# Gates in seven products behind the attention's projection, and a state-space layer cut into tables and a main part

## The chip, the cores and the metric

The kernel runs on one core of a Trainium2 chip. TensorE (PE) multiplies matrices into PSUM; VectorE (DVE), ScalarE (ACT) and GpSimd (POOL) do the elementwise work; transfers are issued from the queues of SP, ACT and POOL. Every engine takes its instructions in the order in which the program emits them, and waits on semaphores for what other engines produce. The metric is the time of one execution in microseconds of the device. Before the change it is 2796.81 us, the median of 3 runs (2796.46 to 2797.84).

## The reference

One decoder block in float32. 16 learned tokens are put before 512 tokens of width 2048, so 528 rows go in and 512 come out.

```python
n = rms_norm(h, norm_mix[l])
z = n @ w_in[l]
q_lat, kv_lat, k_r, u, gates = jnp.split(z, [OFF_Q, OFF_KV, OFF_KR, OFF_U], axis=-1)
...
attn_out = attn @ w_attn_proj[l]
y = s5_scan(u.reshape(bsz, length, SSM_GROUPS, SSM_GROUP), ...)
y = jax.nn.gelu(y.reshape(bsz, length, SSM_WIDTH).astype(h.dtype))
ssm_out = (y @ w_glu_val[l]) * jax.nn.sigmoid(y @ w_glu_gate[l])
mixed = jax.nn.sigmoid(g[:, :, 0]) * attn_out + jax.nn.sigmoid(g[:, :, 1]) * ssm_out
h = h + mixed @ w_out[l]
m = rms_norm(h, norm_ffn[l])
h = h + (jax.nn.silu(m @ w_ffn_gate[l]) * (m @ w_ffn_up[l])) @ w_ffn_down[l]
```

The widths that matter here: u has 1024 columns, q_lat and kv_lat 512 each, the rotated key 64 (128 in the kernel's form), the gates 4096. The attention has 16 heads; the state-space layer has 64 groups of 16 channels and 64 complex states. The output is the final norm of h without the learned tokens.

## The kernel before

**Precision and units.** Activations and weights are each split into a high and a low part (`hilo`, L317; `Weights._split`, L261 and L262), ScalarE making the high part and VectorE the low one. A product is three matmuls: high by high, high by low, low by high. Weights come in blocks of 128 x 1024, that is eight k tiles of one column tile, on SP's queue. One block is one unit of TensorE: 8 k tiles x 3 matmuls. `Weights.use` (L279) splits two blocks ahead of TensorE; the parts lie in rings of three buffers, and the blocks as loaded in `wraw`, a ring of three, which in the seven-product stages is joined by H0 to H3 and H6.

**Two forms.** `dense` (L369) is the plain form: 16 k tiles in two units for one column tile. `seven` (L1353) multiplies a 2 x 2 arrangement of half-size blocks with seven products instead of eight: for one column tile of two (512 tokens, 16 k tiles by 2 column tiles) seven units of 24 matmuls with 256 columns, named P1, P5, P6, P2, P7, P3, P4. VectorE builds weight sums for it (`_combine`, L228); the activations are needed in the forms XD, B12, XA, T12 and T34. The first pair of a stage is `plain_pair` (L1509), four units of 24 matmuls with 512 columns or their halves, during which the operands of the sevens are split. `gathered` (L1381) brings the seven products of a pair together.

**Stages.** (1) Input norm and split of x. (2) Eight tiles of u, 528 wide, stored in DRAM (`ud`). (3) Four tiles of kv, one of the rotated key (kr), four of q, then 32 plain tiles of the gates, whose sigmoids go to DRAM (`sg`). (4) The attention, head by head in an order written out by hand (`TURN`). (5) Its projection, 16 plain tiles, each multiplied with its gate. (6) The two GLU products from y, gated and merged. (7) The output projection. (8) The FFN, gate and up in sevens. (9) Down in three parts, two of which begin with a plain pair. (10) The final norm.

**Work beside the matmuls.** `dense` calls `bg` (L354) behind every unit. It first runs what stands in `later` with a count that has come down to zero, and then steps a generator, `ssm` (L510), as long as there is credit: each call adds 3.6 and each step subtracts the cost that it yields. Credit never rises above 3.6. `ssm` makes the state-space layer's parameters and then, for each of four blocks of 16 groups, its tables and its results: a Toeplitz table (`kd`, then TT), the input expansion transposed for TensorE (BT), the rotations (ER), the powers of the output side (CLt), then states, rotation, scan, rotation back, and outputs y, which go to DRAM (`yd`). It starts with kv and is finished by `bg(1e9)` behind the gates. `by_group` (L496) moves halves of a tile between partitions with transfers on ACT's queue.

**What sets the order around the change.** On each engine the order is the emitted one, so a small matmul of `ssm` stands between two units of TensorE, and a waiting instruction holds up all behind it. On POOL's queue stand the transfers of u, y, kd, the gates and the operands; a transfer into a buffer waits until the last reader of what lay there is done. PSUM has two buffers A, two B, and one each of D, Q and V; the attention's first products take them in turns (`up_ps`, L877). The key's rotation needs the transfers kcs and krs, the queries' rotation (`up_rope`, L883) the tables cs.

## Time and profile before

| what | us |
|---|---|
| median of 3 runs | 2796.81 |
| the profiled execution | 2798.5 |
| its span, first to last instruction | 2796.7 |
| TensorE busy | 2753.9 (98%) |
| VectorE busy | 1908.9 (68%) |
| ScalarE busy | 1136.4 (41%) |
| GpSimd busy | 414.5 (15%) |
| first and last gate tile stored | 231.3 and 611.3 |
| attention's projection, first matmul | 906.3 |
| a stretch of the FFN's sevens, 1510 to 2305: TensorE busy | 795.0 of 795 |

Rows of the profile are read so. A group: line, engine, operation, out<-in by tile names, partitions x elements, count, then total busy time and mean ns of one, then the idle time in front of it and what ended it. A row of the chain or the timeline: start, length, what, count. A row of stretches: from and to, length, busy time with count for PE, PEld, DVE, ACT and POOL, then TensorE's granted clock, the share of the DMA engines and GB/s. A row of transfers: out<-in, queue, count, size, time from issue to landing. Matmul durations of one instruction overlap with the next, so the pace of a unit is read from the chain.

### The profile page before, as it was taken

How to read it: one execution, taken by the hardware profiler on the slowest of the kernel's cores; microseconds unless marked ns; L12 is line 12 of the kernel's file. 1: busy time of each engine (PE TensorE's matmuls, PEld its weight loads, DVE VectorE, ACT ScalarE, POOL GpSimd, SP SyncE). 2: the span in 40 equal slices, each digit the busy share in tenths (PEclk: the TensorE clock that was granted, in tenths of full speed). 3: DMA queues.
4: the chain of work that ended last, by engine and by line, in shares of the span. 5: the costliest groups of instructions: out<-in, count | busy, mean ns of one | idle time of the engine just before them, and what ended most of it. 6: DMA issues, size and time to landing. Idle time of an engine off the chain costs nothing.

```text
span 2796.7 us, 47538 instructions
## 1 busy us (share of the span) xinstructions
PE 2753.9 (98%) x19654; PEld 2537.8 (91%) x19654; DVE 1908.9 (68%) x2609; ACT 1136.4 (41%) x1625; POOL 414.5 (15%) x633
## 2 busy tenths in 40 slices
PE   9999999999999999999999999999999999999997
PEld 8988788889998888888889999999999998999997
DVE  6467556556666333343578888888888888788896
ACT  5123222235555332232234444444444445353445
POOL 2012222231111000111212000000000002030202
PEclk9999999999999999999999999999999999999999
DMA  5334454552122343334434434343433336474542
GB/s 193 107 117 118 136 150 118 146 145 69 61 65 61 125 139 112 114 117 143 143 114 140 139 129 151 112 145 129 143 135 122 136 133 253 168 261 167 206 156 99
DMA packets 114632, 378.88 MB, mean 135 GB/s; under 512 B 16720, under 2 KB 21584, under 8 KB 114352
## 3 DMA queue, kind: packets, MB, share of 16 engines
q1 hardware_dynamic: 76672, 263.36, 27.7%
q0 software_dynamic: 36320, 109.29, 12.4%
q10 hardware_dynamic: 1424, 3.21, 0.5%
q8 instruction: 154, 2.52, 0.4%
q14 instruction: 62, 0.51, 0.1%
HBM read 316.04 MB, written 51.97 MB: 132 GB/s over the span
## 4 chain that ended last, share of the span: by engine, by line
PE 91%; DVE 3%; DMA 2%; issue 2%; ACT 1%; POOL 0%; DVEq 0%; ACTq 0%; POOLq 0%
PE psA L315 60%; PE psB L315 19%; PE psQ L315 5%; PE psV L315 4%; PE psD L315 1%; DVE wlo L262 1%; DVE S L322 1%; DMA S<-td 0%; DMA raw<-in_wst 0%; DVE ev L322 0%; PE psA L1028 0%; ACT whi L261 0%; DMA T<-td 0%; DMA ssB<-td 0%; DMA H<-td 0%
## 5 line engine op out<-in xcount | busy, mean ns | idle before, releaser
L315 PE MATMUL psA<-S,whi 128*128 128x256 f32 (+2 forms) x5440 | 1305.6, 327 | 16.9 <-ACT whi L261 6.5
L315 PEld LDWEIGHTS psA<-S,whi 128*128 128x128 f32 x5440 | 920.1, 188 | 115.8 <-ACT whi L261 7.9
L315 PE MATMUL psA<-S,wlo 128*128 128x256 f32 (+2 forms) x2720 | 889.6, 327 | 1.0 <-DVE wlo L262 0.9
L262 DVE TENSOR_TENSOR wlo<-raw,whi 128x1024 fp32r<-128x1024 f32 (+1 forms) x479 | 592.8, 1239 | 296.0 <-ACT whi L261 293.7
L261 ACT ACTIVATE whi<-raw 128x1024 fp32r<-128x1024 f32 (+1 forms) x479 | 504.3, 1055 | 533.9 <-PE psA L315 254.8
L315 PEld LDWEIGHTS psA<-S,wlo 128*128 128x128 f32 x2720 | 512.7, 189 | 48.9 <-DVE wlo L262 1.6
L315 PE MATMUL psB<-S,whi 128*128 128x256 f32 (+1 forms) x1392 | 285.0, 283 | 0.1
L262 DVE TENSOR_TENSOR wlo<-cmb,whi 128x1024 fp32r<-128x1024 f32 x180 | 220.0, 1222 | 67.4 <-ACT whi L261 66.3
L261 ACT ACTIVATE whi<-cmb 128x1024 fp32r<-128x1024 f32 x180 | 190.5, 1058 | 177.6 <-DVE wlo L262 124.9
L315 PEld LDWEIGHTS psB<-S,whi 128*128 128x128 f32 x1392 | 227.2, 189 | 0.3 <-PE psD L315 0.3
L315 PE MATMUL psB<-S,wlo 128*128 128x256 f32 (+1 forms) x696 | 195.9, 281 | 1.6 <-DVE wlo L262 1.6
L315 PEld LDWEIGHTS psB<-S,wlo 128*128 128x128 f32 x696 | 131.5, 189 | 1.8 <-DVE wlo L262 1.8
L1316 POOL DMA_DIRECT2D td<-sC x22 | 15.8, 720 | 755.8 <-ACT ev L1388 711.9
L242 DVE TENSOR_TENSOR cmb<-raw,raw 128x1024 f32<-128x1024 f32 x60 | 73.2, 1219 | 10.5 <-DMA raw<-in_wst 10.5
L322 DVE TENSOR_TENSOR H<-psA,ev 128x512 f32<-128x512 f32 x32 | 22.1, 691 | 85.2 <-PE psA L315 85.2
L840 ACT ACTIVATE ev<-ev 128x512 f32<-128x512 f32 x32 | 20.2, 632 | 147.6 <-DVE ev L322 147.5
L322 POOL TENSOR_TENSOR acc<-acc,ev 128x512 f32<-128x512 f32 (+2 forms) x43 | 53.4, 1241 | 162.6 <-ACT ev L1619 80.6
L315 PE MATMUL psA<-H,whi 128*128 128x264 f32 (+2 forms) x312 | 76.5, 334 | 0.7 <-DVE ev L322 0.5
L242 DVE TENSOR_TENSOR cmb<-cmb,raw 128x1024 f32<-128x1024 f32 x60 | 73.3, 1221 | 0.0
L242 DVE TENSOR_TENSOR cmb<-raw,cmb 128x1024 f32<-128x1024 f32 x60 | 73.2, 1220 | 0.0
L242 DVE TENSOR_TENSOR raw<-raw,raw 128x1024 f32<-128x1024 f32 x60 | 73.1, 1219 | 0.0
L315 PE MATMUL psB<-ssA,whi 128*128 128x256 f32 (+1 forms) x340 | 72.5, 303 | 0.0
(630 smaller groups left out, 4906.7 us busy)
## 6 DMA issues: line engine op xcount, KB each, us to landing
raw<-in_wst SPq DMA_DIRECT2D x485, 512.0 KB, 3.6
td<-sC POOLq DMA_DIRECT2D x22, 512.0 KB, 3.2
td<-H POOLq DMA_DIRECT2D x40, 256.0 KB, 3.3
S<-td POOLq DMA_DIRECT2D x40, 256.0 KB, 7.4
sg<-ev POOLq DMA_DIRECT2D x32, 256.0 KB, 2.3
ev<-sg POOLq DMA_DIRECT2D x32, 256.0 KB, 2.9
U<-ER POOLq DMA_DIRECT2D x64, 64.0 KB, 2.0
ev<-in_xT POOLq DMA_DIRECT2D x16, 256.0 KB, 2.9
```

Of the source, the lines that this page charges most:

```text
L242: self.nc.vector.tensor_tensor(t, g(a), g(b), op=op)
L261: self.nc.scalar.activation(hi[:, a:b], w[:, a:b], AF.Copy)
L262: self.nc.vector.tensor_tensor(lo[:, a:b], w[:, a:b], hi[:, a:b], op=ALU.subtract)
L315: PE.matmul(o, lhsT=l, rhs=r, start=start, stop=stop, skip_group_check=more)
L322: eng.tensor_tensor(o, a, b, op=op)
L840: ACT.activation(e, e, AF.Sigmoid)
L1316: POOL.dma_start(td[pr, 0:2].rearrange("f p n -> p f n"), Cu)
```

## The change

The gates leave the first stages. Their weights move in the stream behind those of the attention's projection, ordered by pairs: the pair of a column tile of the attention's gate and the same tile of the state-space gate. The first pair is plain, the other 15 are sevens. Their operands are made from x again: `x_products` loads x, multiplies with gain and norm factor and stores the forms to DRAM (`xd`), beside the attention's projection. The projection's tiles go to DRAM (`ao`) and are multiplied with their gates in the gates stage.

The state-space layer is cut in two. `ssm_first` makes parameters and tables for all four blocks, with an allowance of 4.0 a unit, from behind the second tile of u on, and keeps them in DRAM (`bd`, `ed`, `kd`, `cd`), but for the last block's powers. C is loaded without its zero columns and multiplied once for all blocks; the first 18 rotations are computed for all blocks at once. What is left of it behind kr is emitted at once by `run_out`. `ssm_main` runs beside the attention's projection with one step a unit: it loads the tables, makes the last powers, and computes states, scan and outputs; the Gelu is applied as the outputs leave PSUM. `bg` now steps a list of generators, each with its own allowance and credit.

The order of the first stages becomes u, q, kv, kr. The kv norm is started behind kr's first unit and all its pieces behind the second; the key's rotation is finished behind the queries' first rotation. The last GLU operands are loaded and split during the last gate pair. In the down projection the first pairs' weights go through the eight raw buffers (kind Q), and all T12 operands are loaded at P6 of the pair before.

`seven`, `gathered`, `plain_pair`, `Operands` and `products` move ahead in the file, with `Operands` taking its source and `products` its destination as arguments. The core of the diff:

```diff
+N_FIRST = 94
+N_GATES = 4 * KT
...
-    it = [("P", b) for b in range(N_PLAIN)]
+    it = [("P", b) for b in range(N_FIRST)] + [("Q", N_FIRST + b) for b in (0, 2, 1, 3)]
+    for q in range(1, N_GATES // 4):
+        it += [("S", N_FIRST + 4 * q, u) for u in range(7)]
+    it += [("P", b) for b in range(N_FIRST + N_GATES, N_PLAIN)]
...
-                it += [("P", d + b) for b in (0, 2, 1, 3)]
+                it += [("Q", d + b) for b in (0, 2, 1, 3)]
...
+            if it[0] == "Q":
+                self.loads.append((i, i, it[1], self.RAW[nraw % 8]))
+                nraw += 1
+            elif it[0] != "S":
...
+        for g in list(bg_gens):
+            g[1] = min(g[1] + g[2], g[2])
+            while g[1] > 0:
+                try:
+                    g[1] -= next(g[0])
+                except StopIteration:
+                    bg_gens.remove(g)
+                    break
+
+    def beside(gen, allow):
+        bg_gens.append([gen, 0.0, allow])
+
+    def run_out():
+        for g in bg_gens:
+            for _ in g[0]:
+                pass
+        bg_gens.clear()
...
+    def ssm_tables(b):
+
+
+        js, g0 = slice(b * BP, (b + 1) * BP), b * BG
+        Bt = sb([P, 2, BP, 16], F32, "sw")
+        POOL.dma_start(Bt, A["sb"][:, :, js])
+        Dg = sb([P, BG * 16], F32, "sK")
+        POOL.dma_start(Dg, A["sd"][:, g0 * 16:(g0 + BG) * 16])
+        T1 = sb([P, 2 * T], F32, "T1")
+        T2 = sb([P, 2 * T], F32, "T2")
+
+        C, C48 = tabs["C"], tabs["C48"]
+        for ph, c in ((slice(0, P), 0), (RH[0], 16), (RH[1], 32)):
+            ACT.activation(C48[ph, :, :, c:c + 16], C[ph, :, js], AF.Copy)
+
+        ER = sb([P, 4, BP, NC_], F32, "ER")
+        for i in range(2):
+            ACT.activation(ER[:, 2 * i, :, :18], tabs["rt"][i][:, js], AF.Copy)
+        POOL.memset(ER[:, 3, :, 0], 0.0)
+        DVE.tensor_copy(ER[:, 3, :, 1:], e8[:, 2, js].unsqueeze(2).to_broadcast([P, BP, NC_ - 1]))
+        yield 0.7
+        for m, k in ((17, 17), (34, 31)):
+            double((ER[:, 0], ER[:, 2]), m, k, BP, T1, T2)
+            yield 1.0 + 0.05 * k
+        ts(ER[:, 1], ER[:, 2], -1.0, None, MUL)
+        POOL.dma_start(ed[b], ER.rearrange("p a j c -> p (a j c)"))
+        yield 0.5
+
+        BL = sb([P, 2, BP, CL * 16], F32, "ssA")
+        yield from expand(BL, Bt, js, 0, 1, T1, T2)
+        yield 1
+
+        pk = ps([P, 512], "Q")
+        for j in range(BP):
+            for i in range(2):
+                for r in RH:
+                    mm(pk[r, j * 32:(j + 1) * 32], BL[:, i, j, r], C48[:, i, j, 16:48], i == 0, i == 1)
+        tt(Dg, pk[:, :BG * 16], Dg, ADD)
+        for i in range(CL):
+            POOL.dma_start(kd[:, g0:g0 + BG, i], Dg[i * 16:(i + 1) * 16].rearrange("p (g o) -> p g o", o=16))
+        yield 0.4
+        BT = sb([P, BP, 2, P], F32, "ssB")
+        for j in range(0, BP, 2):
+            pt = ps([P, 4, P], "B")
+            for i in range(4):
+                PE.transpose(pt[:, i], BL[:, i % 2, j + i // 2], ident)
+            ACT.activation(BT[:, j:j + 2].rearrange("p a b c -> p (a b) c"), pt, AF.Copy)
+            yield 0.1
+        POOL.dma_start(bd[b], BT.rearrange("p j a c -> p (j a c)"))
+        if b == 3:
+            POOL.dma_start(c3, C48.rearrange("p a j q -> p (a j q)"))
+
+    def ssm_powers(b):
+
+        js = slice(b * BP, (b + 1) * BP)
+        C48 = tabs["C48"]
+        T1 = sb([P, 2 * T], F32, "T1")
+        T2 = sb([P, 2 * T], F32, "T2")
+        CLt = sb([P, 2, BP, P], F32, "ssA")
+        yield from expand(CLt, C48, js, 1, -1, T1, T2)
+        for g in range(2):
+            for r in range(2):
+                POOL.dma_start(cd[b, g, r * 64:(r + 1) * 64],
+                               CLt[g * 64:(g + 1) * 64, r].rearrange("p j m -> p (j m)"))
+
+    def ssm_first():
+        yield from ssm_params()
         for b in range(4):
-            j0, g0 = b * BP, b * BG
-            js = slice(j0, j0 + BP)
-            while "kr" in left:
-                yield 3.3
-            Bt = sb([P, 2, BP, 16], F32, "sw")
-            POOL.dma_start(Bt, A["sb"][:, :, js])
-            Ct = sb([P, 2, BP, 48], F32, "sC")
-            POOL.dma_start(Ct, A["sc"][:, :, js])
-            Dg = sb([P, BG * 16], F32, "sK")
-            POOL.dma_start(Dg, A["sd"][:, g0 * 16:(g0 + BG) * 16])
-            U = sb([P, BG, NC_], F32, "U")
+            yield from ssm_tables(b)
+            if b < 3:
+                yield from ssm_powers(b)
...
+        def load_b(b):
+            BT = sb([P, BP, 2, P], F32, "ssA")
+            POOL.dma_start(BT.rearrange("p j a c -> p (j a c)"), bd[b])
+            nxt_["BT", b] = BT
...
+        def load_t(b):
+
+            g0 = b * BG
             TT = sb([P, BG, P], F32, "ssB")
             POOL.memset(TT, 0.0)
             for i in range(CL):
                 s = CL - 1 - i
                 POOL.dma_start(TT[i * 16:(i + 1) * 16, :, s * 16:],
                                kd[:, g0:g0 + BG, 0:i + 1].rearrange("p g t o -> p g (t o)"))
-            yield 1.3
-            CLt = sb([P, 2, BP, P], F32, "ssA")
-            yield from expand(CLt, Ct, 1, -1)
-            C2 = by_group(sb([P, 2, BP * P], F32, "ER"), CLt.rearrange("p a j m -> p a (j m)"))
-            C2 = C2.rearrange("p g (j m) -> p g j m", m=P)
-            yield 3.4
-            Y = sb([P, BG, 64], F32, "T1")
-            pys = [ps([P, BP, 64], "V"), ps([P, BP, 64], "Q")]
+            C2 = [sb([P, BP, P], F32, t) for t in ("H2", "H3")]
+            for g in range(2):
+                POOL.dma_start(C2[g].rearrange("p j m -> p (j m)"), cd[b, g])
+            nxt_["T", b] = TT, C2
...
+        load_u(0)
+        load_e(0)
+        load_t(0)
+        C48 = sb([P, 2, BP, 48], F32, "sC")
+        POOL.dma_start(C48.rearrange("p a j q -> p (a j q)"), c3)
+        tabs["C48"] = C48
+        yield 1
+        for _ in ssm_powers(3):
+            yield 1
+        load_b(0)
+        nxt_["m"] = [sb([P, 2, T], F32, t) for t in ("T1", "T2", "v", "w")]
+        for b in range(4):
+            states(b, 0)
+            rotate(b, 0)
+            if b:
+                outputs(b - 1, 1)
+            yield 1
+            states(b, 1)
+            rotate(b, 1)
+            if b < 3:
+                load_b(b + 1)
+                load_u(b + 1)
+            if b:
+                store(b - 1)
+                load_t(b)
+            yield 1
+            scan(b)
+            yield 1
+            back(b)
+            if b < 3:
+                load_e(b + 1)
+            yield 1
+            outputs(b, 0)
+            yield 1
+        outputs(3, 1)
+        store(3)
...
+        if j == 1:
+            beside(ssm_first(), 4.0)
...
+    acc_kv = sb([P, T], F32, "KS")
     for j in range(4):
         o = halves("A", "B")
         dense(n, KT, o)
+        if j == 0:
+            normed(qn, acc_q, SEQ, 48, 0, 1)
...
+    later.append([1, lambda: normed(kvn, acc_kv, T, 52, 4, 4)])
     dense(n, KT, o)
-    kr = sb([P, T], F32, "U")
+    run_out()
+    krc = sb([P, 2, T], F32, "S1")
+    kr = krc[:, 0]
+    POOL.dma_start(krc[:, 1], A["kcs"])
...
+    def x_products():
+
+        x = {}
+
+        def load(i):
+            x[i] = sb([P, 2, SEQ], F32, ("H1", "H5")[i % 2])
+            POOL.dma_start(x[i], A["xT"][i::8][:, :, META:].rearrange("k p n -> p k n"))
+
+        load(0)
+        yield 2
+        for i in range(8):
+            if i < 7:
+                load(i + 1)
+            for m in range(2):
+                stt(x[i][:, m], x[i][:, m], gv[:, i + 8 * m:i + 8 * m + 1], rstd_x[:, META:], MUL, MUL)
+            t = sb([P, 2, SEQ], F32, "H7")
+            products(xd[i], x[i], t[:, 0], t[:, 1])
+            yield 3.2
+
+    N = Operands(xd, 0, 8)
+    L, S = (lambda kind, *k: lambda: N.load(kind, k)), (lambda kind, *k: lambda: N.split(kind, k))
+    begin = {12: [L("XD", *range(4)), L("XA", *range(4))],
+             13: [S("XD", *range(4)), L("XA", *range(4, 8)), L("B12", 2)],
+             14: [S("XA", *range(4)), L("B12", 3, 0, 1)],
+             15: [S("XA", *range(4, 8)), S("B12", *range(4)), L("T12", *range(8))]}
+    beside(ssm_main(), 1.0)
+    beside(x_products(), 2.2)
     for j in range(KT):
         p = ps([P, 512], "A")
         dense(at, KT, [(p, 0, SEQ)])
-        s_ = nxt
-        if j % 2 == 0:
-            m_ = sb([P, 2, SEQ], F32, f"H{j // 2}")
-        tt(m_[:, j % 2], p, s_, MUL)
-        mr.append(m_[:, j % 2])
-        nxt = mixg(j + 1)
-        if 4 <= j < 12:
-            load_y(j - 4)
-    yl = ym
-
+        t = ev(SEQ)
+        ACT.activation(t, p, AF.Copy)
+        POOL.dma_start(ao[j], t)
+        assert j < 12 or not bg_gens
+        for h in begin.get(j, ()):
+            h()
...
+    plain = [[L("T34", *range(8))], [S("T12", *range(4))], [S("T12", *range(4, 8)), S("T34", 0)],
+             [S("T34", *range(1, 5))]]
+    for j in range(KT):
+        ag = []
+
+        def load_ao():
+            ag.append(sb([P, SEQ], F32, "acc"))
+            POOL.dma_start(ag[0], ao[j])
+
+        if j == 0:
+            C = sb([P, 2, SEQ], F32, "H7")
+            for m, o in enumerate(plain_pair(N.X, plain)):
+                ACT.activation(C[:, m], o, AF.Sigmoid)
+            load_ao()
+        else:
+            hooks = {k: list(v) for k, v in (first if j == 1 else last if j == KT - 1 else {}).items()}
+            hooks["P6"] = hooks.get("P6", []) + [load_ao]
+            C = []
+            seven(N.X, 8, 1, gathered(("H7", "sC")[j % 2], C), hooks)
+            C = C[0]
+            ACT.activation(C, C, AF.Sigmoid)
+        tt(C[:, 0], C[:, 0], ag[0], MUL)
+        POOL.dma_start(sg[j].rearrange("m p n -> p m n"), C)
+    st.free = {"wraw"}
...
-                    "P6": [S("XD", 0, 1, 2, 3), L("T12", 0, 1, 2, 3)],
+                    "P6": [S("XD", 0, 1, 2, 3), L("T12", *range(8))],
                     "P2": [L("B12", 3), S("B12", 2)],
                     "P7": [L("B12", 0, 1)],
                     "P3": [S("B12", 3), L("XA", *range(8))],
-                    "P4": [S("B12", 0, 1), L("T12", 4, 5, 6, 7)]}
+                    "P4": [S("B12", 0, 1)]}
```

706 lines of the change are left out of this document (332 added, 374 removed).

## The prediction

> **What bounds the kernel now.** I read the page's first part, the stretches by engine, the chain of waits, and then the groups of the stages that the change touches.
>
> ```profile
> span 2796.7 us, 47538 instructions
> PE 2753.9 (98%) x19654; PEld 2537.8 (91%) x19654; DVE 1908.9 (68%) x2609; ACT 1136.4 (41%) x1625; POOL 414.5 (15%) x633
> ```
> ```profile
> 250.00:605.00 355.00, 352.82 (x2340) 288.28 (x2339) 214.28 (x334) 98.06 (x122) 92.28 (x163) 1.00 0.49 138
> 1510.00:2305.00 795.00, 795.00 (x6773) 794.03 (x6772) 665.05 (x702) 369.55 (x464) 37.36 (x62) 1.00 0.38 133
> 2350.00:2355.00 5.00, 2.16 (x19) 1.96 (x17) 5.00 (x8) 2.29 (x4) 0.74 (x1) 1.00 0.39 152
> 2355.00:2360.00 5.00, 4.35 (x26) 4.38 (x27) 5.00 (x8) 1.58 (x2) 0.72 (x1) 0.72 0.62 210
> 2360.00:2365.00 5.00, 5.00 (x43) 5.00 (x42) 5.00 (x8) 2.65 (x3) 0.00 (x0) 0.94 0.47 165
> ```
> TensorE is the bound: it is busy in the whole gates stage (250 to 605) with the state-space work beside it, and in the whole seven-product stage (1510 to 2305). So removed matmuls are time, state-space matmuls cost the same wherever they stand, and each new wait of TensorE is lost in full. The last three rows show what else a wait costs: it is followed by a lower granted clock.
>
> **The gain: 15 pairs of gates.** From the chain in order of time (start, length, what):
>
> ```profile
> 33.27 5.83 PE psD L315 x48
> 1090.99 5.58 PE psB L315 x24
> 1509.95 5.64 PE psA L315 x48
> 2298.92 5.64 PE psA L315 x48
> 2368.61 5.65 PE psA L315 x48
> 2466.91 5.65 PE psA L315 x48
> 2531.94 5.64 PE psA L315 x48
> ```
> A plain unit (24 matmuls, 512 columns; 48 of 264 for the 528-wide tiles of u, kv and kr, 5.8) takes 5.58 us, a pair of gate tiles four units, 22.32. The rows of x48 are P4 of one seven and P1 of the next; between 1509.95 and 2298.92 lie 40 sevens, 19.72 each. VectorE was busy 665 of 795 us there with more work per pair than gates have, so I take 19.72: 15 x 2.60 = **39.0 us gained**. The first pair stays plain.
>
> The same rows price the two entries of the down projection. The last seven before it begins at 2298.92 + 2.82 and ends 19.72 later, at 2321.46; the plain pair and the next seven end at 2371.43: 49.97 where 42.04 would do, 7.9 lost. From 2466.91 in the same way 45.31, 3.3 lost. The change loads these plain weights through the eight raw buffers and the T12 operands earlier. Bounds 0 and 11.2; part of this is operand traffic that stays, so I take **5 gained**.
>
> **Cost 1: into the attention.** The tables' generator has 30 calls of 4.0 left after the second tile of u, 120, and its steps add up to 131.6. What is left goes out in one piece before the next matmul: both halves of the last block's expansion, the small matmuls that read it, the transposes. These stand ahead of the attention in TensorE's order. VectorE in the same stretch of before:
>
> ```profile
> L262 DVE TENSOR_TENSOR wlo<-raw,whi 128x1024 fp32r<-128x1024 f32 x82 | 101.9, 1247 | 108.8 <-ACT whi L261 108.6 <-PE psA L315 0.3
> L322 DVE TENSOR_TENSOR ssA<-T,T 128x1024 f32<-128x1024 f32 x16 | 19.6, 1225 | 0.5
> L322 DVE TENSOR_TENSOR T<-sw,spw 128x1024 f32<-128x1024 f32 x16 | 18.8, 1218 | 0.0
> L322 DVE TENSOR_TENSOR T<-ER 128x256 f32<-128x256 f32 x16 | 6.1, 421 | 0.2
> L322 DVE TENSOR_TENSOR T<-ER 128x128 f32<-128x128 f32 x16 | 3.9, 286 | 0.2
> L325 DVE SCALAR_TENSOR_TENSOR ev<-ssA,gv,acc 128x528 f32<-128x528 f32 x4 | 3.0, 760 | 0.0
> L319 DVE TENSOR_TENSOR H<-ev,H 128x528 fp32r<-128x528 f32 x4 | 2.8, 709 | 2.8 <-ACT H L318 2.8
> L322 DVE TENSOR_TENSOR ssA<-psA,rstd 128x264 f32<-128x264 f32 x4 | 1.7, 431 | 4.1 <-PE psA L315 4.1
> L322 DVE TENSOR_TENSOR ev<-ev,acc 128x528 f32<-128x528 f32 x2 | 1.4, 708 | 0.8 <-ACT acc L403 0.8
> L318 ACT ACTIVATE H<-ev 128x528 fp32r<-128x528 f32 x4 | 2.6, 646 | 7.9 <-DVE ev L325 7.9
> L329 DVE TENSOR_SCALAR ER<-ER 128x528 f32<-128x528 f32 x4 | 1.7, 432 | 0.2
> ```
> Queued on VectorE from the end of the first kr unit: the kv norm's factor (two scalings 0.43, ScalarE's root 0.65, three passes at 0.71 and one at 0.43, some 0.6 for the ones matmul), 4.7; the second half of the third block's powers, 1.22 + 1.22 + 1.23 = 3.7; a weight's low part 1.25; the four kv pieces, each 0.76 + 0.70 waiting for ScalarE + 0.71, 8.7; the last block's doublings, 6 x 0.29 + 6 x 0.42 + 0.43 + a copy of the same size, 5.1; the expansion 2 x 3.67, 7.3. Together 30.8. TensorE has the ones matmuls (1.2) and the second kr unit (5.8), 7.0. **Wait 24 us**; it is at least 8 if all but the expansion ran ahead, and 30 if VectorE arrives late.
>
> Then the tables for the queries' rotation:
>
> ```profile
> 332.87 2.06 PE L315 MATMUL psQ<-sC,ssA 128*64 128x32 f32 x64
> 334.86 1.09 PE L681 MATMUL psB<-ident,ssA 128*128 128x128 f32 x8
> 615.76 1.29 DVE L322 TENSOR_TENSOR ev<-psA,sC 128x512 f32<-128x512 f32 x2 [0.69 <-DMA sC<-in_cs]
> 617.10 0.51 PE L315 MATMUL psA<-H,whi 128*128 128x264 f32 x2 [0.48 <-DVE ev L322]
> T<-in_kcs POOLq DMA_DIRECT2D x1, 264.0 KB, 3.0
> sC<-in_cs POOLq DMA_DIRECT2D x1, 512.0 KB, 3.8
> ```
> Their load now stands on GpSimd's queue behind eight stores of kd, bd, c3, the load of kcs and the krs transfer, which waits for VectorE's product with kcs. Counted from the small matmuls' start: kd can go at 2.5, eight issues 4.5, three more 1.7, kcs lands 3.0 after its issue, the product 0.7, krs 0.6, cs lands 3.8 later, two products 1.3: about 17.5. TensorE needs that PSUM buffer back after 2.1 + 2.3 (transposes) + 5.6 (rotation) + 1.45, at 11.4. **Wait 6**, between 0 and 10; before, this same wait was 0.48.
>
> **Cost 2: kv.** In the eight kv units VectorE has 8 x 1.25, four evacuations of 0.86, the q norm 12.4 (as kv's, with ScalarE's turns) and 28 of tables (3.7 and 7.3 of block 1; 5.1, 7.3 and 3.7 of block 2; small ones 0.9), 54; TensorE 8 x 5.8 = 46.4 and twice 2.1 + 2.3 of small matmuls, 55. Nearly even, and the small matmuls read fresh expansions: **5**, between 0 and 10.
>
> **Cost 3: the attention's projection.** Rows of before at its start, and of transfers:
>
> ```profile
> 906.30 0.50 PE L315 MATMUL psA<-S,whi 128*128 128x512 f32 x1 [1.20 <-ACT S L318]
> 905.62 2.19 ACT L318 ACTIVATE S<-ssA 128x512 fp32r<-128x512 f32 x4
> 908.69 2.49 DVE L319 TENSOR_TENSOR S<-ssB,S 128x512 fp32r<-128x512 f32 x4
> L325 DVE SCALAR_TENSOR_TENSOR ev<-w,gv,acc 128x512 f32<-128x512 f32 x2 | 1.5, 746 | 0.0
> L740 POOL DMA_DIRECT2D ssB<-kd x32 | 17.8, 563 | 1.2 <-POOL ssB L737 1.2
> L737 POOL MEMSET ssB<- 128x2048 f32 x4 | 7.3, 1832 | 0.0
> td<-sC POOLq DMA_DIRECT2D x22, 512.0 KB, 3.2
> sg<-ev POOLq DMA_DIRECT2D x32, 256.0 KB, 2.3
> w<-v ACTq DMA_DIRECT2D x8, 132.0 KB, 3.3
> ```
> The ssB buffer is free at 911.2. GpSimd then has its memset 1.8, eight loads 4.5, three more 1.7, and only then the first x tile: issued at 919.2, landed at 922.4. VectorE stands before it, since the x product (two of 0.75, four of 0.42: 3.2) is ahead of the low weights of unit 3, which come at 926.8 where TensorE wants them at 906.3 + 3 x 5.58 = 923.0: **4 us**, 0 to 5. Then powers 3.7, low 1.2, powers 3.7, x product 3.2: 938.6. GpSimd first sends that product's stores (to 939.7), then four powers (942), which land 2.3 after; only then is ssA free for bd, 1 MB, for which I take 4.5 from 512 KB in 3.2: 948. The first state matmuls stand behind unit 3, which ends at 932.4: **wait 16**, 9 to 20. What a wait there holds up is all of TensorE.
>
> For each block the step back through VectorE and the two copies through DRAM (3.3 after issue), and GpSimd's 27 issues of 0.56 plus memset, 17 us, are set against three units and small matmuls, some 18: about 2 each for three blocks, **6**, 0 to 12. The last output has no x product beside it.
>
> **Cost 4: into the gates.** ScalarE first copies tile 15, which waits for its last matmul, then splits four XA and B12 0 to 3; the plain pair reads B12 2 after three matmuls. Seven and a bit of ScalarE's 0.55 to 0.6 plus VectorE's 0.62 (2.49 for four above): **5**, 3 to 7. The operands of T12 and T34 are covered by the plain pair's 22 us. At the GLU four y splits are left: **1**, 0 to 3.
>
> **Cost 5: the clock.** The rows 2355 to 2365 lose 0.28 x 5 + 0.06 x 5 = 1.7 us of clock behind a wait. For the three longest waits (24, 16, 5): **5**, between 3 and 9.
>
> The Trainium skill, TensorE: Matmul & The Clock Gate, section Part 1: The HAM clock gate, says that an idle window of about 3.4 us halves the clock until about 3.4 us of work have passed, so a gap costs some 1.7 us whatever its length, which agrees with the 1.7 of the row. By that threshold, an estimate, the waits of 4 and 6 us would pay too: 8.5 in place of 5.
>
> **Sum:** -39 - 5 + 24 + 6 + 5 + 4 + 16 + 6 + 5 + 1 + 5 = **+28**. The profiled execution took 2798.5 us with its span of 2796.7; the median is 2796.8. So 2826.5 for such an execution and **2825** for the median, the likeliest case's own range being 2806 to 2845.
>
> **Rivals.**
> Faster: the handovers are met because VectorE's queue runs ahead of TensorE, so that only the work issued last is waited for. Then 8 is left at the attention and 9 at the first state matmuls, 3 at the gates, 4 of clock, nothing else, and both down entries recover: 39 + 11 - 24 = 26, about 2771. It decides once VectorE has 16 us less ahead of the expansion than I count. For it: before, TensorE hardly waited beside nearly the same work. Against: then all of the expansion had two units' lead, and the rows add up to 30.8 against 7.
>
> GpSimd becomes the bound in the projection: its 17 us per block, the x stores and the stores of the projected tiles share one queue, so each of the last three blocks is 8 late instead of 2: 2825 + 18 = 2843. For it: SP does not share its load. Against: before it was 15% busy, and the x stores end with block 1.
>
> Gates fall behind 19.72 because ScalarE's sigmoid (1024 columns) delays weights: at 21.0 a pair the gain is 20, about 2844. Against: 370 of 795 us ScalarE busy in the same form.
>
> **How the numbers follow.** Forecast 0.60, faster rival 0.23, GpSimd 0.10, slow gates 0.03, all but cancelling 0.04. About 0.2% (5.6 us) is what a measurement of this kernel tells from no change. Faster 0.23, same 0.04, slower 0.73. The range 2778 to 2848 holds the forecast, most of the two slow rivals and the slower third of the faster one; the bounds of all terms at once would give 2770 to 2864.
>
> **What would show it.** A gap of some 24 us on TensorE ahead of the small matmuls psQ<-U,ssA of the last block; one of about 16 ahead of psD<-U,ssA in the projection; one of 5 in the first gates unit, waiting for B12; low granted clock behind each; 19.7 between gate sevens. I am wrong if TensorE enters the attention without a long wait, or if the gates' pace is above 20.

## The result, and the profile after

The changed kernel takes 2892.5 us (median of 4 runs, 2889.3 to 2894.7) against 2797.3 for the kernel before (2796.5 to 2799.1): a ratio of 1.0338, with a 95% interval of 1.0326 to 1.0350. The sign was as forecast, the size was not: +95 where +28 was forecast, and outside the range. The page's first part after the change:

```profile
span 2892.9 us, 50212 instructions
PE 2759.4 (95%) x20782; PEld 2603.3 (90%) x20782; DVE 2049.5 (71%) x2690; ACT 1217.5 (42%) x1766; POOL 478.7 (17%) x731
```

TensorE was idle for 2796.7 - 2753.9 = 42.8 us before and for 2892.9 - 2759.4 = 133.5 after: 90.7 us of new waits. What ended them, by the view of TensorE's waits (total, how many, the longest):

```profile
PE psQ L316 <- DVE ssA L323: 26.6, 3, 20.2
PE psD L316 <- DMA ssA<-bd: 18.0, 1, 18.0
PE psV L316 <- DMA ssB<-kd: 17.0, 2, 8.9
PE psA L316 <- DVE ev L323: 14.7, 2, 8.0
PE psA L316 <- DVE wlo L263: 7.9, 1, 7.9
...
PE psB L710 <- ACT ssB L711: 5.1, 8, 0.7
PE psA L316 <- ACT acc L1271: 4.0, 1, 4.0
...
PE psV L316 <- DMA H<-v: 1.9, 1, 1.9
```

The predicted places are all there: 20.2 ahead of the last block's small matmuls, 18.0 ahead of the first state matmuls, 4.0 at the gates' entry. New are 6.7 us in u (the other part of psA <- ev beside 8.0) and 5.1 at the transposes; 17.0 on kd stand where 6 were forecast for all outputs.

The chain of waits has the sevens of the gates, and those around the first entry of the down projection (start, length):

```profile
892.25 5.66 PE psA L316 x48
...
1149.65 5.66 PE psA L316 x48
...
2395.00 5.66 PE psA L316 x48
...
2460.87 5.69 PE psA L316 x48
```

Thirteen gate sevens take 257.40, 19.80 each. From 2395.00 to 2460.87 are 65.87 for a plain pair and two sevens (62.12): 3.8 us lost where 7.9 were.

The stretch from 1700 to 2300 us holds only sevens of gate and up, the same instructions in both kernels (the numbers behind PE's busy time are matmuls). First before, then after:

```profile
1700.00:2300.00 600.00, 600.00 (x5116) 599.40 (x5115) 501.70 (x530) 278.72 (x349) 26.07 (x43) 1.00 0.38 133
```
```profile
1700.00:2300.00 600.00, 600.00 (x5067) 599.83 (x5066) 499.17 (x528) 276.14 (x347) 27.09 (x45) 1.00 0.38 132
```

At full clock, with TensorE never idle, 1% fewer matmuls were done: a seven of gate and up takes 19.90 instead of 19.72. The prediction had nothing of this kind.

Where the 95 us are, against the terms of the prediction:

| term | forecast | measured | from |
|---|---|---|---|
| 15 gate pairs | -39.0 | -37.7 | the run with plain gates, below |
| waits, with the down entries' -5 | +62 | +90.7 | idle time of TensorE |
| lower clock | +5 | +27.5 | busy time x (1 - granted clock), summed over stretches of 5 us up to 900 |
| pace of matmuls by place | 0 | +11 | the run with a 128-byte pad, below |
| sum | +28 | +91.5 | (95.2 by the medians; 3.7 not assigned) |

### The profile page after: what moved, and what is told of

It is laid out like the page before. It is cut to its first block, busy times and chain, and to the rows that moved or that the text cites. A ratio compares the mean times of both kernels' runs of the same rounds, so it can differ in the third digit from the quotient of the medians.

```text
span 2892.9 us, 50212 instructions
## 1 busy us (share of the span) xinstructions
PE 2759.4 (95%) x20782; PEld 2603.3 (90%) x20782; DVE 2049.5 (71%) x2690; ACT 1217.5 (42%) x1766; POOL 478.7 (17%) x731
## 4 chain that ended last, share of the span: by engine, by line
PE 86%; DVE 6%; DMA 3%; issue 2%; ACT 1%; POOL 1%; DVEq 0%; SPq 0%; ACTq 0%; POOLq 0%
PE psA L316 50%; PE psB L316 22%; PE psQ L316 6%; PE psV L316 5%; PE psD L316 2%; DVE wlo L263 1%; DVE T L323 1%; DVE ev L323 1%; DVE S L323 1%; DMA H<-in_xT 1%; DMA ssA<-bd 0%; PE psB L710 0%; POOL ssB L766 0%; PE psA L1123 0%; ACT whi L262 0%
## 5 line engine op out<-in xcount | busy, mean ns | idle before, releaser
L316 PE MATMUL psA<-S,whi 128*128 128x256 f32 (+2 forms) x5136 | 1124.3, 309 | 20.8 <-DVE ev L323 6.7
L316 PEld LDWEIGHTS psA<-S,whi 128*128 128x128 f32 x5136 | 845.4, 190 | 76.5 <-issue 10.2
L316 PE MATMUL psA<-S,wlo 128*128 128x256 f32 (+2 forms) x2568 | 791.5, 308 | 7.9 <-DVE wlo L263 7.9
L263 DVE TENSOR_TENSOR wlo<-cmb,whi 128x1024 fp32r<-128x1024 f32 x225 | 274.8, 1221 | 96.4 <-ACT whi L262 95.3
L316 PE MATMUL psB<-S,whi 128*128 128x256 f32 (+1 forms) x1632 | 330.3, 284 | 0.5 <-ACT ssB L711 0.5
L262 ACT ACTIVATE whi<-cmb 128x1024 fp32r<-128x1024 f32 x225 | 237.7, 1056 | 201.5 <-DVE wlo L263 121.6
L316 PE MATMUL psA<-H,whi 128*128 128x512 f32 (+2 forms) x448 | 120.4, 355 | 8.9 <-DVE ev L323 8.0
L316 PEld LDWEIGHTS psA<-H,whi 128*128 128x128 f32 x448 | 78.2, 192 | 19.9 <-DVE ev L323 8.2
L1250 ACT ACTIVATE ev<-psA 128x256 f32<-128x256 f32 x114 | 43.4, 381 | 100.7 <-PE psA L316 100.7
L316 PE MATMUL psA<-H,wlo 128*128 128x512 f32 (+2 forms) x224 | 78.0, 348 | 0.0
```

The lines of the kernel that those rows point to most:

```text
L262: self.nc.scalar.activation(hi[:, a:b], w[:, a:b], AF.Copy)
L263: self.nc.vector.tensor_tensor(lo[:, a:b], w[:, a:b], hi[:, a:b], op=ALU.subtract)
L316: PE.matmul(o, lhsT=l, rhs=r, start=start, stop=stop, skip_group_check=more)
L1250: ACT.activation(snap[name], o, AF.Copy)
```

## The experiments

All start from the changed kernel (2892.5) unless another start is named; the kernel before ran beside each group, at 2796.9 to 2798.1.

### The gates alone (e_plain)

```diff
-    for q in range(1, N_GATES // 4):
-        it += [("S", N_FIRST + 4 * q, u) for u in range(7)]
+    for q in range(N_GATES // 4):
+        it += [("P", N_FIRST + 4 * q + b) for b in (0, 2, 1, 3)]
...
+            for m, o in enumerate(plain_pair(M.X, hk)):
+                ACT.activation(C[:, m], o, AF.Sigmoid)
```

> The changed kernel with the gates computed by plain products: all 16 pairs of tiles like the first one, on the same operands, with no T12 and T34 loads; everything else of the change stays. Theory: the seven-product form earns what the traces say, 15 pairs of 22.32 against 19.80, so this is 37.8 us slower than the change, about 2930. Rival: the form's operand loads, splits and combinations cost TensorE something outside its own pace, so that less than 30 us is lost.

Measured 2930.3, 37.7 above the change. The gain is there in full; what failed is all beside it.

### The place of the operands (e_pad, e_align, e_align2, e_dist, e_before)

The groups of the profile don't show it, but the intervals between matmul starts do. In the seven's stretch, medians in ns by moving operand (under high weights; T stands for two tiles, T1 and T2):

```
operand          ER   ssA  ssB  T    v    S
before           113  114  113  117  114  119
after            118  118  118  117  118  119
128-byte pad     113  114  113  116  114  119
operands at 32   120  120  120  120  120  120   (in threes of 123, 117, 120)
... weights 96   114  114  114  114  114  114
```

The change allocates some small tables earlier, and this moves ER, ssA, ssB and v by some kilobytes, from 32 to 160 above a multiple of 256 bytes.

```diff
     cf = sb([P, 2, 32], F32, "scf")
+    sb([P, 32], F32, "pad")
```

> One unused tile of 128 bytes is put ahead of the evacuation buffers, so that all tiles behind it lie 128 bytes higher; no instruction changes. Theory 'place': the pace of a 256-column matmul depends on where its moving operand starts in SBUF. In the traces of before and after, tiles whose start is 32 above a multiple of 256 bytes run at about 113 ns a matmul, the others at 116 to 120. In the changed kernel ER, ssA, ssB, v start 160 above such a multiple (118 ns); with the pad they start 32 above it. Then their matmuls take 113 to 114 ns, the sevens of gate and up fall from 19.90 to about 19.7 us, those of the gates from 19.80 to about 19.6, and with 75 sevens at 0.18 the time falls by 8 to 14 us, to about 2881. Theory 'traffic': the sevens are slower because of the transfers or the weights beside them. Then the pad changes nothing (2892.5, within 2 us).

Measured 2881.4, 11 less; the matmuls of these tiles went back to 113 to 114 ns, 5118 in the stretch. So an allocation cost 11 us, with no instruction to show for it.

e_align moves all operand tiles to 32 above a multiple of 256 (two pads of 64 bytes, and a view that starts 128 bytes into the tile):

```diff
+    def pairtile(tag):
+        c = 32 if tag in OFF else 0
+        return sb([P, 2 * T], R, tag)[:, c:c + 2 * SEQ].rearrange("p (a n) -> p a n", a=2)
```

> The changed kernel with two unused tiles of 64 bytes, and with the operand tiles of the gates, the projections and the sevens starting 128 bytes into their space where that brings them to 32 above a multiple of 256; no instruction is added or removed. Theory 'place': all these tiles then run at 113 to 114 ns for 256 columns, also the S tiles that have never stood there (119 ns). A seven falls from 19.9 to about 19.1, which is 55 to 60 us over 75 sevens; if the 512-column matmuls gain the same 5 ns each, another 10. The time is 2825 to 2838. Theory 'tile, not place': S tiles stay at 119 ns and the gain is that of the 128-byte pad, to about 2881.

Both theories fell: 2906.5, slower by 14, and every operand at 120 ns. One of the pads had moved the weights too, from 96 to 160. e_align2 puts only those back:

```diff
         if k == 0:
+            sb([P, 48], F32, "pad2")
             st.split(1)
+            sb([P, 16], F32, "pad3")
```

> As the run with the operand places, where the whole projection of tiles ran at 120 ns; there the two pads had also moved the ring of high and low weights, from 96 above a multiple of 256 to 160. Two more unused tiles (192 and 64 bytes) put the weights back to 96 and leave the operands at 32. Theory 'distance': what counts is the operand's start less the weights' start, modulo 256. 192 was fast (113 ns) in the traces of before and of the 128-byte pad; 0, 64 and 128 were slow (117 to 120). Now all tiles have 192: a seven falls to about 19.1 and the time by 55 to 70 us, to 2822 to 2838. Rival 'operand count': the fast pace needs some tiles to differ from others, and with all alike the matmuls stay at 120 ns, about 2905.

Measured 2859.6, 33 less than the change, about half of what was expected. The same stretch of the two runs, e_align first:

```profile
1700.00:2300.00 600.00, 600.00 (x5002) 600.00 (x5002) 492.86 (x522) 271.68 (x342) 27.09 (x45) 1.00 0.38 131
```
```profile
1700.00:2300.00 600.00, 599.52 (x5197) 597.40 (x5196) 510.25 (x540) 284.59 (x357) 27.09 (x45) 1.00 0.39 136
```

3.9% more matmuls in the same time, with the operands where they were modulo 256 and the weights moved by 192 bytes. The Trainium skill, TensorE: Matmul & The Clock Gate, Part 2, section Step-by-step: what each phase is for, has two independent read ports for the moving operand and for the weights, so that loading weights takes nothing from the running matmul. These two runs show a price that this doesn't foresee: the weights' place alone decides about 4% of the pace. Whether it is their loading into TensorE or their writing by ScalarE and VectorE that depends on the place, the runs don't separate.

e_dist leaves the operands and moves the weights from 96 to 32 (the same two pads, without the rest):

> The changed kernel with 192 unused bytes ahead of the ring of high and low weights and 64 behind it: the weights start 32 above a multiple of 256 instead of 96, the operands stay where they are. Theory 'distance' (operand less weights is 192 modulo 256 in every fast case so far): the even S tiles (224) now have distance 192 and run at 113 to 114 ns, the odd S tiles (96) and ER, ssA, ssB, v (160) stay at 117 to 120; 2870 to 2885. Theory 'both at fixed places' (weights at 96 and operand at 32): nothing is at its place and all tiles run at 117 to 122 ns, 2890 to 2910.

Measured 2884.4. The time is in the first theory's range, the paces are not: the even S tiles ran at 116 to 117, the odd ones at 118 (averages; the first two aside), where 113 to 114 and 117 to 120 were expected. "Distance" orders the cases only roughly. It also can't say why the even S tiles ran at 116 before and at 119 after on unchanged places, both weights and operand. Nor is 32 enough by itself: T2 before and after the change, and w after it, also start at 32 above a multiple of 256, with the weights at 96, and ran at 115 to 116 on average. That place sets the pace is shown; by which rule is open.

e_before gives the kernel before the places of e_align2:

> The kernel before, with nothing of the change, but with its operand tiles and weights at the places of the second place run (operands at 32, weights at 96 above a multiple of 256). If the pace comes from the places alone, its matmuls of 117 to 120 ns fall to 114 to 115 too: a seven from 19.72 to about 19.25, 60 sevens, and some more in the plain products: 2765 to 2772, under both kernels. If the gain of the place runs depended on something in the change, within 5 us of 2797.

Measured 2783.9, a ratio to the kernel before of 0.9952 (0.9938 to 0.9966). Half of the expected gain again, and no part of the change is needed for it:

```profile
1700.00:2300.00 600.00, 599.32 (x5218) 596.87 (x5218) 510.66 (x538) 286.83 (x361) 31.76 (x52) 1.00 0.40 137
```

### Into the attention (e_allow, e_late, e_entry, e_entry2, e_warm)

```diff
-            beside(ssm_first(), 4.0)
+            beside(ssm_first(), 5.0)
```

> The allowance of the tables' generator is 5.0 instead of 4.0 for each weight unit, so that its 131.6 of steps are issued before the end of kr. Theory 'late issue': the 20.2 us wait ahead of the last block's small matmuls comes from what run_out issues in one piece. Then that wait falls under 5 us, the broken transposes and the low clock behind it go, and the attention's first matmul comes at about 250 in place of 276.6: 20 to 30 us less, about 2867. Theory 'VectorE is full': the steps issued earlier only delay the evacuations and the weights' low parts in the same stretch. Then the wait moves to psA<-DVE ev or wlo, and the gain is under 8 us.

Measured 2882.5, 10 less, between the two. The 20.2 became 6.4, but other blocks' small matmuls now waited too (2.5, 1.3 and 3.3 us), and 2.6 and 6.0 us of waits stood at the queries' first matmuls. So part of it was late issue.

The wait in u, by the change's timeline of VectorE: the parameter steps begin right behind the norm's factor, and the first evacuation follows them.

```profile
44.80 0.17 DVE L332 TENSOR_SCALAR sw<-sprm 128x32 f32<-128x32 f32 x1
...
48.11 1.22 DVE L263 TENSOR_TENSOR wlo<-raw,whi 128x1024 fp32r<-128x1024 f32 x1
...
52.77 0.62 DVE L323 TENSOR_TENSOR ev<-psA,rstd 128x264 f32<-128x264 f32 x1
```

```diff
-        if j == 1:
+        if j == 2:
             beside(ssm_first(), 5.0)
```

> As the run with allowance 5.0, and the generator starts after the evacuations of the first three tiles of u instead of before them. Theory: the 6.70 us wait of TensorE on the evacuation at 46.8 to 53.5, and the 5.7 us at half clock behind it, come only from the parameter steps that stand ahead of these evacuations on VectorE. Then both go and the time is about 9 us under that of the run with the allowance alone. Rival: the two units of lead that are given up come back as wait at the end of kr, since 28 calls of 5.0 are 140 against 131.6 of steps. Then the difference is under 3 us either way.

Measured 2875.2, 7.3 less; the 6.70 is gone and TensorE is 63.9 of 64 us busy at full clock from 46 to 110. The theory holds, a little of the gain coming back as other waits.

e_entry gives the small matmuls more lead. It starts from e_late:

```diff
+        yield from ssm_er(0)
         for b in range(4):
...
         yield from expand(BL, Bt, js, 0, 1, ...)
-        yield 1
+        if b < 3:
+            yield from ssm_er(b + 1)
+        else:
+            yield 4
```

> As the run with allowance 5.0 and the late start, and the rotation table of the next block is made between an expansion and the small matmuls that read it (so these have some 5 us of VectorE work as lead), with the queries' rotation table loaded ahead of the key's. Theory 'lead': the 12.4 us that TensorE still waits for psQ<-U,ssA in four pieces, with the low clock behind each, come from small matmuls issued right behind the expansion that they read. Then these waits fall under 4 us together and the time is about 2860, 15 under the run with the late start. Theory 'VectorE is full' (29 to 33 of 40 us busy there): the same wait reappears at evacuations and low weights, and the time stays within 5 us of 2875.

Measured 2887.4, 12 more than e_late. The waits for the expansion did fall, from 12.4 to 5.2, but the reordering brought the load of the next block's B table right ahead of its first reader, and VectorE waited for it, with ScalarE's high weights and TensorE behind it (19.2 us in four pieces):

```profile
162.91 2.36 DVE L323 TENSOR_TENSOR T<-sw,spw 128x1024 f32<-128x1024 f32 x2 [6.68 <-DMA sw<-in_sb]
```

e_entry2 issues that load a step earlier:

```diff
     def ssm_er(b):
+        tabs["Bt"] = sb([P, 2, BP, 16], F32, "sw")
+        POOL.dma_start(tabs["Bt"], A["sb"][:, :, js])
```

> As the run with lead for the tables, in which VectorE stood idle for 6.68 and 7.05 us until a block's B table had landed, because its load was issued only right ahead of the expansion, and ScalarE and TensorE stood behind VectorE. Here that load is issued one step earlier. Theory 'order': these two waits go and with them the 6.3 and 3.8 us waits of TensorE on high weights; the time is about 2862, under the late start's 2875. Theory 'VectorE is full': other waits take their place and the time is 2872 or more.

Measured 2877.3, on the side of "VectorE is full". VectorE's wait is gone, and TensorE now waits 6.3 us for a PSUM buffer that the kv evacuation holds, and 3.8 for the copies of the transposes. With VectorE 30.8 of 40 us busy between 190 and 230 in a queue in order, lead for one reader is delay for another.

e_warm asks what the lower clock comes from. Nobody reads the added result:

```diff
+        if b == 3:
+            pv_ = ps([P, 512], "V")
+            for i in range(86):
+                mm(pv_, n[1][:, 0, :P], n[0][:, 0, :512], True, True)
         pk = ps([P, 512], "Q")
```

> The changed kernel with 86 additional matmuls of 512 columns on operands that are already there, whose result nobody reads, ahead of the last block's small matmuls, where TensorE waits 20.2 us. They need 19.9 us. Theory 'idle': the low clock from 245 to 300 us (0.53 of full speed between 245 and 277) comes from the idle wait, so that with TensorE kept busy it stays at 1.0 and the time falls by 6 to 10 us, to about 2884. Theory 'small work': the low clock comes from the 32-column matmuls and transposes that follow; then nothing is gained, 2892 or more.

Measured 2894.2: nothing gained. Stretches of the change (PE busy first, the granted clock third from the end):

```profile
245.00:255.00 10.00, 0.00 (x0) 0.00 (x0) 7.33 (x10) 2.34 (x4) 3.04 (x6) 0.61 0.51 157
...
265.00:270.00 5.00, 1.87 (x32) 1.74 (x34) 3.44 (x3) 0.00 (x0) 0.00 (x0) 0.50 0.11 44
270.00:275.00 5.00, 4.31 (x48) 3.85 (x45) 1.10 (x3) 0.77 (x2) 2.29 (x5) 0.50 0.11 10
275.00:280.00 5.00, 5.00 (x21) 4.08 (x20) 0.00 (x0) 4.39 (x16) 3.85 (x7) 0.72 0.55 136
```

and of e_warm:

```profile
245.00:255.00 10.00, 10.00 (x44) 8.10 (x44) 7.17 (x9) 2.54 (x5) 3.04 (x6) 1.00 0.51 159
...
265.00:270.00 5.00, 1.75 (x36) 1.64 (x32) 3.28 (x3) 0.00 (x0) 0.00 (x0) 0.75 0.07 29
270.00:275.00 5.00, 4.31 (x45) 3.85 (x44) 1.10 (x3) 0.94 (x2) 2.46 (x5) 0.50 0.12 9
275.00:280.00 5.00, 5.00 (x21) 4.05 (x20) 0.00 (x0) 4.26 (x16) 3.69 (x7) 0.73 0.57 152
```

With TensorE kept busy through the long wait the clock is full until 265 and then falls all the same, to 0.50 while TensorE is 4.3 of 5 us busy with 32-column matmuls and transposes. It comes back with the 512-column matmuls after 275. From 265 to 280 busy time x (1 - granted clock) is 3.9 us instead of 4.5.

A second wait stands ahead of most of these matmuls in both runs (3.1 us, and 3.2 in e_warm), and the added matmuls don't fill it. In the kernel before, the same 64 matmuls of 32 columns and 16 transposes ran from 208.1 to 212.6, right behind dense matmuls and with a wait of 0.25 us among them:

```profile
205.00:210.00 5.00, 5.00 (x78) 4.13 (x76) 1.49 (x2) 0.00 (x0) 0.00 (x0) 1.00 0.61 203
210.00:215.00 5.00, 4.75 (x36) 3.94 (x33) 4.29 (x27) 2.17 (x4) 4.05 (x8) 1.00 0.30 30
```

So this small work alone doesn't bring the clock down; a wait ahead of it has a part. And other small matmuls bring it back: in the change, 64-column matmuls follow the 8.1 us wait on kd, from 754.3 to 758.9, and the clock is full again before 760:

```profile
755.00:760.00 5.00, 4.59 (x65) 4.33 (x66) 0.00 (x0) 1.08 (x3) 0.00 (x0) 0.59 0.80 325
760.00:765.00 5.00, 5.00 (x31) 3.84 (x31) 1.23 (x1) 0.95 (x2) 0.55 (x1) 1.00 0.44 152
```

The Trainium skill, TensorE: Matmul & The Clock Gate, Part 4: PE-mode transpose, says that the full clock doesn't engage for transposes, which don't count as busy in the same way; the row from 270 to 275 is in line with it. Whether the 32-column matmuls count, these runs don't separate.

### Beside the projection (e_proj, e_proj2, e_proj3)

```diff
-            BT = sb([P, BP, 2, P], F32, "ssA")
+            if b == 0:
+                BT = [sb([P, 4, 2, P], F32, t) for t in ("KS", "H6")]
...
+                outputs(b - 1, 1)
+                load_t(b)
             yield 1
...
-    beside(ssm_main(), 1.0)
     beside(x_products(), 2.2)
+    beside(ssm_main(), 1.0)
```

> Only the state-space work beside the attention's projection is rearranged: the first block's bd goes into two free tiles (KS, H6) at the start instead of waiting for ssA, the x load stands ahead of the state-space loads on GpSimd's queue, and each kd table load is issued one unit earlier, ahead of the stores. Theory 'order': the 18.0 us wait of psD on bd, the 7.9 on the low weights and the 17.0 on kd come from the order of issues. Then all three fall under 3 us each, and with the clock behind them the projection (584 to 847, 263 us) shortens by 40 to 50, to about 2847. Theory 'GpSimd or the DMA engines are full': between 640 and 700 the DMA engines were 0.87 busy and GpSimd's queue half. Then the waits only move to a later load, and the gain is under 25 us.

Measured 2897.2, 5 more than the change: the theory of the order alone fell. The waits named are gone or smaller, another took their place:

```profile
PE psV L316 <- DMA H<-v: 25.1, 2, 22.6
...
PE psD L316 <- issue: 8.0, 2, 4.6
PE psA L316 <- DVE wlo L263: 6.6, 2, 6.2
...
PE psV L316 <- DMA yd<-H: 6.0, 1, 6.0
```

GpSimd's timeline in the change shows what the queue does. The eighth U load doesn't read bd and uses no tile of it, and still it stands until that transfer, issued eight places ahead, has landed:

```profile
645.91 0.54 POOL L751 DMA_DIRECT2D ssA<-bd  x1 [1.55 <-PE psD L316]
646.47 3.94 POOL L745 DMA_DIRECT2D H<-ud  x7
655.02 0.56 POOL L745 DMA_DIRECT2D H<-ud  x1 [4.61 <-DMA ssA<-bd]
```

e_proj2 relieves that queue:

```diff
-                POOL.dma_start(U[i * 16:(i + 1) * 16],
+                nc.sync.dma_start(U[i * 16:(i + 1) * 16],
...
-        POOL.dma_start(ao[j], t)
+        ACT.dma_start(ao[j], t)
...
+                outputs(b - 1, 0)
                 outputs(b - 1, 1)
```

> As the run that rearranged the projection, and in addition: the U loads go to SyncE's queue, the stores of the projected tiles to ScalarE's, the first x product comes one unit after its load, and both output groups of a block stand at the next block's first step. Theory 'GpSimd's queue': in that run the waits only moved (22.6 and 2.5 us ahead of psV<-H,H, 4.6 and 3.4 ahead of psD, 6.3 on wlo) because issues on GpSimd's queue stood idle until a transfer that they don't read had landed (the eighth U load waited 0.70 for an xd store; in the kernel of the change 4.61 for ssA<-bd). With fewer transfers there, all waits of TensorE in the projection add up to less than 10 us and the time is about 2850. Theory 'DMA engines': the transfers themselves are what is slow (0.87 busy), whichever queue issues them. Then 25 us or more of waits stay and the time is above 2875.

Measured 2882.7 with 37 us of waits on transfers (U 17.7, the state's H<-v 10.8, weights 8.9): by its own numbers the side of "DMA engines". But the edit also issues the next block's U and bd loads one step later, behind the scan, so that the waits for U can be late issue as well; e_best4 below bears on this. e_proj3 spreads the x products:

```diff
-    beside(x_products(), 2.2)
+    beside(x_products(), 1.35)
```

> As the second rearranged projection (2882.7; 37 us of waits on transfers, the DMA engines 0.93 busy between 640 and 700), but the x products are spread over 23 units of the projection instead of 12, so that their 12 MB or so move at about half the rate. Theory 'DMA engines': landings in the first half come sooner (a 256 KB xd store took 7.4 us there) and the waits of psD and psV fall from 37 to under 15: about 2858. Theory 'order of issues': the waits stay where they are, 2878 or more.

Measured 2871.2, 11.6 less, between the two; 28 us of waits ahead of the state matmuls stayed.

### Together (e_best, e_best2, e_best4, e_best3)

e_best joins e_entry, e_proj2, e_align and the B12 splits ahead of the copy:

> Everything together: the lead for the tables, the rearranged projection with its queues, the operand places, and the splits of B12 ahead of ScalarE's copy of the last projected tile (which takes away the 4.0 + 0.8 us at the gates' entry). If the parts are separate terms they add up: 2892.5 - 32 - 42 - 60 - 5, about 2753, under the kernel before by 44. If a later wait takes the place of an earlier one, it is above 2790.

Measured 2877.5 instead of 2753: it carried the poor places of e_align and the late table load of e_entry. With the parts as measured (+14.0, -5.2, -9.8 and about -5) the sum is 2886.5.

e_best2 joins e_late, e_proj3, e_align2 and the splits:

```diff
+        for h in begin.get(j, ()):
+            h()
         t = ev(SEQ)
         ACT.activation(t, p, AF.Copy)
-        for h in begin.get(j, ()):
-            h()
```

> Together: the late start with allowance 5.0 (-17.3 against the change), the projection with x products spread and queues moved (-21.3), the operand places with the weights at 96 (-32.9), the splits of B12 ahead of ScalarE's copy (-4.8 of waits), the queries' table first. If the terms are separate: 2892.5 - 76 = about 2816, still above the kernel before. If they share a cause (VectorE, the DMA engines), above 2830.

Measured 2804.5 (1.0032 of the kernel before, 1.0008 to 1.0055), 12 better than the sum (some of it in the pace, at 113 ns instead of the 114 of e_align2). So the terms don't take from each other, and the 4.0 at the gates' entry is gone with the order of the splits.

e_best4 loads each block's U one block ahead and the bd of even blocks three units earlier:

```diff
+        load_b(1)
+        load_u(1)
...
+            if b < 2:
+                load_b(b + 2)
```

> As e_best2 (2804.5), whose projection still waits 23.0 us for U (H<-ud, twice 11.7 or less) and 7.4 for bd: here each block's U is loaded one block ahead, and the bd of the even blocks goes into two tiles of its own, so that it is loaded three units earlier. Theory 'late issue': the three waits go, with some clock behind them: about 2775, under both kernels. Theory 'DMA engines' (0.80 to 0.90 busy there): an earlier issue moves the wait to another transfer; above 2793.

Measured 2792.2 (0.9983, 0.9972 to 0.9993). Of the 30 us of waits 2.6 are left, and one of 7.3 is new. The time is 12.3 lower, not 30, and lies just under the 2793 of "DMA engines", so by itself it doesn't decide. The landings tell more. Issues between 584 and 735 us (count, size, median from issue to landing), in the change:

```profile
raw<-in_wst SPq DMA_DIRECT2D x16, 512.0 KB, 5.3
...
xd<-H POOLq DMA_DIRECT2D x16, 256.0 KB, 3.9
ssA<-bd POOLq DMA_DIRECT2D x4, 1024.0 KB, 7.4
```

and in e_best4:

```profile
raw<-in_wst SPq DMA_DIRECT2D x20, 512.0 KB, 7.3
...
xd<-H POOLq DMA_DIRECT2D x16, 256.0 KB, 9.8
```

Landings are longer and the DMA engines fuller (0.96 busy from 640 to 700, where it was 0.87), yet TensorE waits less. So fuller DMA engines did not by themselves make TensorE wait longer: the lead had been shorter than the landings, and with more lead even longer landings are met.

e_best3 adds lead for the small matmuls before the attention:

```diff
-        yield 1
+        yield 6
...
-            beside(ssm_first(), 5.0)
+            beside(ssm_first(), 5.5)
```

> As e_best4, and before the attention the small matmuls of each block stand one more weight unit behind the expansion that they read (allowance 5.5 to make up for it). Theory 'lead': the 14.1 us of psQ<-U,ssA in four pieces and half of the 18 us of low clock there go: 20 under e_best4. Theory 'VectorE is full': evacuations or weights are late in their place, and the time is within 5 us of e_best4 or above it.

Measured 2789.2 (0.9965, 0.9953 to 0.9978), 3 under e_best4, which is within the spread of both (2785.8 to 2799.7 and 2784.3 to 2793.2): again the side of "VectorE is full". Its waits for psQ <- ssA are nearly gone and others stand in their place:

```profile
PE psB L714 <- ACT ssB L715: 8.8, 6, 3.8
PE psA L316 <- DVE ev L323: 7.1, 2, 6.7
...
PE psQ L316 <- POOL KS L323: 5.5, 1, 5.5
```

This version of the change is faster than the kernel before as it stood. The kernel before at the same places took 2783.9 (ratio 0.9938 to 0.9966), and the two intervals overlap, so which of them is faster isn't shown. As far as these runs can tell, the 37.7 us that the gates gain are spent again.

## Why the prediction was wrong

**The gain** held: 19.80 a pair by the chain, 37.7 by undoing it. **The down entries** too: 3.8 and, from 2560.37 to 2625.22 in the same way, 2.7 where 7.9 and 3.3 had been lost, 4.7 regained of the 5 forecast. **Cost 4** held: 4.0 and 0.8 against 5, by the mechanism named. The 1 at the GLU did not appear.

**Cost 1** held in its place and size, 20.2 and 3.1 against 24, and 8.0 against 6 for the rotation tables. What it missed lies around it: the 5.1 at the transposes, which wait for ScalarE's copies, and the 6.7 in u. The parameter steps were on VectorE's queue in the listing, and the prediction counted them only as part of the generator's 131.6, not as something queued ahead of an evacuation. e_late shows that they were the cause. The 5 of **Cost 2** came as 3.2.

**Cost 3** was mis-sized in two of its three terms: 18.0 against 16 at the first state matmuls, but 7.9 against 4 at the low weights and 18.9 (17.0 on kd, 1.9 on the states) against 6 at the outputs. The wait of 8.9 and 8.1 in two blocks is what the rival "GpSimd becomes the bound" gave for each of three; I had given it 0.10. The landings were taken from stretches of the kernel before in which the DMA engines were 0.38 to 0.49 busy (3.2 us for 512 KB, 2.3 for 256 KB, an estimate of 4.5 for 1 MB). Here they were 0.59 to 0.87 busy, and by the medians an x tile of 512 KB took 6.6, 256 KB 3.9 and 1 MB 7.4.

**Cost 5** is the term that failed most: 5 forecast, between 3 and 9, and 27.5 measured. It failed in the number of places and in the price of one. I counted the three longest waits at 1.7 us each; the clock was at half in nine places up to 900 us, and each lost 1.3 to 5.4 us, 3.1 on average. The 1.7 came from the rows behind one wait of 3.5 us. With dense matmuls behind them, waits of 6.7, 8.0 and 7.9 us lost 3.1, 3.0 and 2.8, and the 4.0 us at the gates' entry 1.3. The largest losses, 5.4 and 4.5, stand where 32-column matmuls and transposes follow a wait of 3.2 us and the waits of 20.2 and 3.1; e_warm shows that filling the 20.2 alone saves almost nothing. What sets the price of a place is not shown beyond that. The rule of the Trainium skill weighed there (TensorE: Matmul & The Clock Gate, Part 1: The HAM clock gate), some 1.7 us a gap whatever its length, gives 8.5 for five gaps and, an estimate, 15.3 for nine, and both fall short.

**The pace**, the assumption that TensorE's matmuls cost the same wherever they stand, failed by 11 us (e_pad). No row of the prediction could have shown it, but the trace of before had tiles at 113 and at 119 ns for the same instruction, and the change did move them.

**The faster rival** (VectorE runs ahead) is excluded: TensorE waited 20.2 us at the last block where it left 8, and with all steps issued in time (e_allow, e_best3) waits for VectorE remain in another place. All bounds at once gave 2864, still below the result: the clock's bound was too narrow, and place and u were not in the list.

## What to carry to other kernels

When work is moved beside a dense stretch, count the waits that it makes, and price the lower clock behind each by a wait as long and with the same work behind it: here 1.3 us behind a wait of 4.0 and some 3 behind 7 to 8, with dense matmuls after them, and up to 5.4 where 32-column matmuls and transposes followed. Take landing times from a stretch as crowded as the new one, and give loads that much lead; an in-order queue that is three quarters busy gives lead to one reader at the cost of another, so removing a single wait often only renames it. When a change allocates tiles in another order, compare the spacing of the same matmuls in an untouched stage before explaining anything else.

## What the runs showed of the hardware that was not expected

The spacing of 256-column matmuls at full clock, with nothing waited for, lies between 113 and 120 ns (medians by operand) by where the moving operand and the weights start in SBUF. Moving only unused bytes took this kernel from 2892.5 to 2859.6 or to 2906.5, and the kernel before from 2797.4 to 2783.9. A good pair was all operands at 32 and the weights at 96 above a multiple of 256 bytes; the rule behind it is open.

An issue on GpSimd's queue waited for a transfer eight issues ahead that it had nothing to do with (4.61 us), so one 1 MB load holds up the small loads behind it.
